# The order of the two halves in the last update of x behind the mixer, and in the squares of the norm that follows

## The chip, the cores and the metric

The kernel runs on one core of a Trainium2 chip. The metric is the device time of one execution in microseconds (us); for the kernel before it is the median of three runs. Everything is float32 or the rounded float32 format (fp32r) that the matrix engine takes.

A core has five engines, each with its own instruction stream, run in the order in which it was built: TensorE (PE in the profile; its weight loads stand as PEld), VectorE (DVE), ScalarE (ACT), GpSimd (POOL) and SyncE (SP), which here issues nearly all DMAs. They wait for one another through semaphores. Matrix products land in PSUM, which has eight banks of 128 x 512 float32; everything else lies in SBUF.

## What is computed

One decoder layer on x (1 x 512 x 1024), in three phases. Each one norms x, runs a block, norms its output, and adds that to x:

```
x = x + 0.5 * PostNorm_a(SwiGLU_1(PreNorm_a(x)))
x = x +       PostNorm_b(W_out [HGRN2_heads(h) ; mLSTM_heads(h)]),  h = PreNorm_b(x)
x = x + 0.5 * PostNorm_c(SwiGLU_2(PreNorm_c(x)))

def rms_norm(x, g):
    xf = x.astype(jnp.float32)
    y = xf * lax.rsqrt(jnp.mean(xf * xf, axis=-1, keepdims=True) + EPS)
    return (y * g.astype(jnp.float32)).astype(x.dtype)

def swiglu_ffn(x, w_in, w_out):
    gate, up = jnp.split(x @ w_in, 2, axis=-1)
    return (jax.nn.silu(gate) * up) @ w_out
```

The change lies where the second phase ends and the third begins: PostNorm_b, the addition to x, PreNorm_c, and the first products of SwiGLU_2.

## The kernel before

**Tiles and precision.** The 512 rows of x are four chunks of 128, held in SBUF as `xs` (128 x 4 x 1024). A chunk's row of 1024 is worked on in two halves of 512: half 0 is columns 0 to 511, half 1 is columns 512 to 1023. Every matrix operand is split into a rounded high part and a remainder: a cast on ACT writes the high part and a subtraction on DVE the rest (lines 245 and 247 for weights, 339 and 341 or 353 and 352 for the normed x). A product is then three matmuls, high by high and the two mixed ones.

**The end of the mixer.** Its output product has two column halves. The first (`mix_out0`) runs for all four chunks, and `post0` leaves its result, times the gain of PostNorm_b, in SBUF as `y` (line 443), with the squares of the first half summed. The second (`mix_out1`) runs chunk by chunk into four banks, `acc[0]` to `acc[3]`. When a chunk's bank is full, `last` (line 468) calls for it, in this order:

1. `post1` (line 446). ACT squares the bank and sums it (line 406, `junk<-ps`). POOL adds this to the sum of half 0 (407) and takes the power -0.5 (411): this is the column `r`. DVE multiplies the bank by the gain in place (453). Then DVE updates x twice (457): half 0 from `y`, which lies in SBUF, and half 1 from the bank, each as x + r * value.
2. `norm(i, 2)`, which is `pre` (414) with `root` (421) and `scaled` (431). ACT squares the two halves of the new x (406, `junk<-xs`) one after the other into the same scratch tile `junk`, POOL makes the root of each sum of squares (407, 407, 411), and DVE scales the two halves by root and gain (433) into `xn` or, for odd chunks, into a part of `hf`.
3. The transposes of the normed chunk on PE (319) and the split of their result into high part and remainder. Those of chunk 0 and chunk 1 are put into the product of chunk 3, those of chunks 2 and 3 into the first products of the third phase (`ffn_head`, line 619).

**The first products of the third phase.** They stand in the list `HEADS`: c1, c3, c2, c4, p1, e1 and so on. c1 to c4 take the first 256 rows, which are chunks 0 and 1; e1 is the first to take chunks 2 and 3. Each is 24 matmuls (line 562). All PSUM tiles come from one ring of eight banks, so a new tile has the bank of the tile eight allocations before it. From `acc[0]` on these are the four `acc`, the four tiles of the transposes of chunks 0 and 1, then c1's, two for the transposes of chunk 2, and c3's.

**Who sets the order.** The code is recorded as a program in which each engine's instructions are put into a sequence by a scheduler of the framework, from the dependences and from what `issue_after` (in `behind`, line 461) forbids. Only the very start of the kernel is written in a fixed order. `post1` and `pre` leave the names of their last square, last update and last scaling in `self.added` and `self.normed`; `ffn_head` puts some weight splits and copies behind them.

`ffn_out` of both SwiGLUs calls `last` too. There `out` is given (a part of `hf`), so neither half is read from a bank in the update, and the norm is called with row 1 or not at all.

Of the kernel before, what the change touches and what calls it, by code (L numbers as in the profile page):

```python
# [87 lines left out]
class Layer:  # L88
# [322 lines left out]
        self.pow = nc.gpsimd.tensor_tensor(r, b, self.nhalf[:, :1], op=ALU.pow)  # L411
        yield r

    def pre(self, i, g):

        r, xn = self.root(i)
        for h in range(2):
            self.scaled(i, g, r, xn, h)
        return xn

    def root(self, i):

        x = self.xs[:, i, :]
        *_, r = self.rms([x[:, :512], x[:, 512:]])
        if i % 2:
            xn = self.hf[:, 16:18, :].rearrange("p a t -> p (a t)")
        else:
            xn = self.sp.tile([P, D], F32, tag="xn", bufs=1, name=self.nm("xn"))
        return r, xn
# [16 lines left out]
    def post1(self, i, y, parts, rms, pieces, g, out=None):  # L446

        nc = self.nc
        for ps, v in pieces:
            parts.append(ps)  # L450
            next(rms)
            o = ps if out is None else out[:, v]
            nc.vector.tensor_tensor(o, ps, g[:, 512 + v.start : 512 + v.stop], op=ALU.mult)
        r = next(rms)
        for h, v in enumerate((y, pieces[0][0] if out is None else out)):
            x = self.xs[:, i, 512 * h : 512 * h + 512]
            added = nc.vector.scalar_tensor_tensor(x, v, r, x, op0=ALU.mult, op1=ALU.add)
        self.added = [self.square, added]
# [1182 lines left out]
def layer(tc, aps):  # L1641
    with ExitStack() as ctx:
        L = Layer(ctx, tc, aps)
        nc = tc.nc
        x, out = aps["x"], aps["out"]
        pre, post = aps["norm_pre"][0], aps["norm_post"][0]
        L.weights(
            L.ffn_items("f1", aps["ffn1_w_in"][0], aps["ffn1_w_out"][0]) + L.mix_items()
            + L.ffn_items("f2", aps["ffn2_w_in"][0], aps["ffn2_w_out"][0])
        )  # L1650
        gp, xn, roots = [None], [None] * NT, {}

        def norm(i, row=None):
            if i == 0 and row is not None:
                gp[0] = L.gain("gpre", pre[row : row + 1, :])
            xn[i] = L.pre(i, gp[0])

        def root(i):

            if i < 2:  # L1660
                norm(i, 1)
            else:
                roots[i] = L.root(i)

        def scaled(i, h):
            r, xn[i] = roots[i]
            L.scaled(i, gp[0], r, xn[i], h)

        def trans(i):
            L.to_t(i, xn[i])  # L1670

        def trans_s(i):
            L.to_s(i, xn[i])

        def store(i):
            for h in range(2):
                v = slice(512 * h, 512 * h + 512)
                nc.sync.dma_start(out[0, i * P : (i + 1) * P, v], L.xs[:, i, v])

        with ExitStack() as f1:  # L1680
            L.open_ffn(f1)
            with tc.manual_schedule():
                first = L.start_loads()
                gp[0] = L.gain_pe("gpre", pre[0:1, :])
                for i in range(NT):
                    for h in range(2):
                        v = slice(512 * h, 512 * h + 512)
                        (nc.scalar if i < 2 and h else nc.sync).dma_start(L.xs[:, i, v], x[0, i * P : (i + 1) * P, v])
                    if i:
                        L.load(first.popleft())  # L1690
                    if i == 1:

                        nc.scalar.activation(L.col(), L.nhalf[:, :1], AF.Exp)
                while first:
                    L.load(first.popleft())
                L.start(norm, xn)
            L.small_params()
            L.ffn_in()
            L.ffn_out(post[0:1, :], 0.5, root, trans, lambda trans: L.head4(trans, scaled))
        L.mixer()  # L1700
        with ExitStack() as f2:
            L.open_ffn(f2)
            L.mix_out1(lambda i: norm(i, 2), trans_s, L.ffn_head)
            L.ffn_in()
            L.ffn_out(post[2:3, :], 0.5, store, lambda i: None, lambda trans: None)
# [30 lines left out]
```

## Time and profile before

| what | value |
| --- | --- |
| median of the runs | 943.95 us (943.27, 943.95, 944.35) |
| the profiled execution | 944.65 us |
| its span, first to last instruction | 942.9 us |
| mean granted clock of PE | 0.999 |
| matmuls | 7507, busy 934.1 us |
| busiest other engine | DVE, 779.7 us |
| output updates of x from a bank (line 457, `xs<-ps`) | 4, at 592.2 to 610.9 us |

The times of the profile are those of one execution, counted from its first instruction. In a row of the timeline stand the start, the duration, the engine, the line in the kernel, the operation, what is written and read, the count of merged instructions, and in brackets the idle time ahead of it with what ended it. In a row of the table of windows each engine has its busy time and the number of its instructions, in the order PE, PEld, DVE, ACT, POOL; then follow the granted clock of PE, the share of the DMA engines, and GB/s. A row of the chain of waits holds the start, the time that the piece adds to the chain, the engine, and what it writes. Matmul ends are modelled, and successive ones overlap in the rows, so their starts say more than their durations.

### The profile page before, as it was taken

The numbers are of one execution on the slowest core, as the hardware profiler recorded it, in microseconds if no ns is written. First come the engines' busy times: TensorE is split into PE (matmuls) and PEld (weight loads), VectorE is DVE, ScalarE is ACT, GpSimd is POOL, SyncE is SP. The second block draws the span as 40 slices with busy tenths as digits, with TensorE's granted clock in tenths as the row PEclk, the third lists the DMA queues.
The fourth block names the chain that finished last, engine by engine and source line by source line (L and its number), as shares of the span: only waits on it lengthen the run. The fifth ranks groups of instructions, "written<-read, shape, count | busy, mean of one in ns | idle before, by whom it ended". The sixth has DMA issues, their size and how long they took to land.

```text
span 942.9 us, 18101 instructions
## 1 busy us (share of the span) xinstructions
PE 934.1 (99%) x7507; PEld 900.4 (95%) x7507; DVE 779.7 (83%) x1056; ACT 490.8 (52%) x695; POOL 120.9 (13%) x176
## 2 busy tenths in 40 slices
PE   9999999999999999999999999999999999999997
PEld 7999999999999999998887888899999999999997
DVE  6799989999888876698846665689998999998884
ACT  7645444456456467956632444664444444655541
POOL 2530000000001046200011310363100000000101
PEclk9999999999999999999999999999999999999999
DMA  9244333323352024321212124324333333223212
GB/s 318 86 135 134 110 116 113 112 90 90 99 171 90 24 85 126 107 67 47 88 46 67 46 90 140 103 71 132 115 113 106 119 113 112 68 90 128 75 46 90
DMA packets 81677, 96.13 MB, mean 102 GB/s; under 512 B 4117, under 2 KB 61497, under 8 KB 81594
## 3 DMA queue, kind: packets, MB, share of 16 engines
q1 hardware_dynamic: 81306, 94.44, 31.7%
q8 instruction: 59, 0.97, 0.4%
q10 hardware_dynamic: 288, 0.52, 0.2%
q14 instruction: 24, 0.20, 0.1%
HBM read 92.85 MB, written 2.10 MB: 101 GB/s over the span
## 4 chain that ended last, share of the span: by engine, by line
PE 62%; ACT 1%; DVE 1%; POOL 0%; issue 0%; POOLq 0%; DVEq 0%; ACTq 0%
PE ps L562 22%; PE ps L835 8%; PE ps L496 6%; PE ps L151 5%; PE ps L843 5%; PE ps L153 4%; PE ps L152 4%; PE ps L1226 2%; PE ps L506 1%; PE ps L319 1%; PE ps L1400 0%; PE ps L1311 0%; PE ps L1480 0%; PE ps L1507 0%; PE ps L1266 0%; ACT junk L406 0%
## 5 line engine op out<-in xcount | busy, mean ns | idle before, releaser
L245 ACT CAST w<-raw 128x1024 fp32r<-128x1024 f32 (+1 forms) x232 | 239.1, 1035 | 252.9 <-PE ps L562 102.5
L247 DVE TENSOR_TENSOR w<-raw,w 128x1024 fp32r<-128x1024 f32 (+1 forms) x232 | 286.1, 1240 | 35.8 <-ACT w L245 35.5
L562 PE MATMUL ps<-xq,w 128*128 128x256 f32 x2016 | 238.5, 277 | 0.0
L562 PEld LDWEIGHTS ps<-xq,w 128*128 128x128 f32 x2016 | 233.8, 188 | 0.2 <-ACT hf L589 0.2
L562 PE MATMUL ps<-sq,w 128*128 128x256 f32 x1440 | 170.5, 277 | 0.0
L562 PEld LDWEIGHTS ps<-sq,w 128*128 128x128 f32 x1440 | 166.8, 188 | 0.0
L835 PE MATMUL ps<-w,hs 128*128 128x256 f32 x1056 | 124.2, 276 | 0.0
L835 PEld LDWEIGHTS ps<-w,hs 128*128 128x128 f32 x1056 | 121.7, 188 | 0.0
L261 DVE TENSOR_TENSOR raw<-raw,raw 128x1024 f32<-128x1024 f32 x64 | 82.3, 1285 | 0.6
L151 PE MATMUL ps<-w,xq 128*128 128x512 f32 x192 | 78.9, 411 | 0.1
L152 PE MATMUL ps<-w,xq 128*128 128x512 f32 x192 | 74.8, 390 | 0.0
L153 PE MATMUL ps<-w,xq 128*128 128x512 f32 x192 | 74.8, 391 | 0.0
L407 POOL TENSOR_SCALAR col<-col 128x1 f32<-128x1 f32 x24 | 9.0, 374 | 493.7 <-ACT junk L406 493.6
L496 PE MATMUL ps<-xq,w 128*128 128x256 f32 x480 | 56.4, 278 | 0.0
L496 PEld LDWEIGHTS ps<-xq,w 128*128 128x128 f32 x480 | 55.2, 188 | 0.5 <-issue 0.5
L843 PE MATMUL ps<-w,hs 128*128 128x256 f32 x432 | 51.9, 276 | 0.0
L261 POOL TENSOR_TENSOR raw<-raw,raw 128x1024 f32<-128x1024 f32 x16 | 44.2, 2763 | 50.7 <-DVE w L247 41.4
L843 PEld LDWEIGHTS ps<-w,hs 128*128 128x128 f32 x432 | 50.3, 188 | 0.0
L754 ACT CAST hs<-hf 128x1024 fp32r<-128x1024 f32 x34 | 35.7, 1050 | 25.7 <-PE ps L843 14.1
L151 PEld LDWEIGHTS ps<-w,xq 128*128 128x128 f32 x192 | 36.1, 188 | 8.2 <-issue 0.9
L153 PEld LDWEIGHTS ps<-w,xq 128*128 128x128 f32 x192 | 36.0, 188 | 8.2 <-DVE xq L326 0.3
L755 DVE TENSOR_TENSOR hs<-hf,hs 128x1024 fp32r<-128x1024 f32 x34 | 41.6, 1224 | 1.5 <-ACT hs L754 1.5
(255 smaller groups left out, 1167.1 us busy)
## 6 DMA issues: line engine op xcount, KB each, us to landing
raw<-in_ffn_w_in_dram SPq DMA_DIRECT2D x88, 512.0 KB, 3.6
raw<-in_ffn_w_out_dram SPq DMA_DIRECT2D x44, 512.0 KB, 4.1
raw<-in_w_mix_in_dram SPq DMA_DIRECT2D x28, 512.0 KB, 3.6
raw<-in_w_mix_out_dram SPq DMA_DIRECT2D x8, 512.0 KB, 3.6
out_dram<-xs SPq DMA_DIRECT2D x8, 256.0 KB, 2.0
xs<-in_x_dram SPq DMA_DIRECT2D x6, 256.0 KB, 7.0
gpost<-in_norm_post_dram SPq DMA_DIRECT2D x3, 512.0 KB, 4.6
gpre<-in_norm_pre_dram SPq DMA_DIRECT2D x2, 512.0 KB, 4.0
```

The source lines that it names most:

```text
L151: mm(ps, sh, mh, start=start, stop=False, **kw)
L152: mm(ps, sh, ml, start=False, stop=False, **kw)
L153: mm(ps, sl, mh, start=False, stop=stop, **kw)
L245: nc.scalar.copy(hi, raw)
L247: self.low = nc.vector.tensor_tensor(lo, raw, hi.bitcast(F32), op=ALU.subtract)
L261: (nc.vector if late else nc.gpsimd).tensor_tensor(o, o, c, op=ALU.add)
L496: mm(ps[:, u0:u1], w[:, a, k, :], self.xop(k, b, u0, u1), start=k + n + m == 0, stop=k == ND - 1 and n == 2, skip_group_check=True,)
L562: self.nc.tensor.matmul(ps[:, c], wb[b][:, k, v], left[d][:, k, :], start=first and a + n + k == 0, stop=n == 2 and k == KH - 1, skip_grou ...
L754: self.nc.scalar.copy(hi, src)
L755: self.nc.vector.tensor_tensor(lo, src, hi.bitcast(F32), op=ALU.subtract)
L835: mm(out, a[kk][:, i * P : (i + 1) * P], w[:, b, kk, QUARTER * v : QUARTER * (v + 1)], start=begin and c == kk == n == 0, stop=kk == 1 and ...
L843: mm(ps[:, QUARTER * c : QUARTER * (c + 1)], A[a][:, c], B[b], start=begin and c == n == 0, stop=n == 2, skip_group_check=True,)
```

## The change

The second of the two updates in `post1` and the first square in the norm behind it trade places with their neighbours, where the update reads a bank. In `post1`, with no `out` given, the half in the bank (half 1) stands first in the code and the half in SBUF second. The norm in front of the third phase, and only this one (row 2), lists half 1 first among its squares. What is computed is the same sum in the other order of its two parts; no instruction is added or removed. The name kept in `self.added` is now that of the update of half 0, and in `self.normed` that of the square of half 0.

```diff
-    def pre(self, i, g):
+    def pre(self, i, g, turned=False):
 
-        r, xn = self.root(i)
+        r, xn = self.root(i, turned)
...
-    def root(self, i):
+    def root(self, i, turned=False):
 
         x = self.xs[:, i, :]
-        *_, r = self.rms([x[:, :512], x[:, 512:]])
+        parts = [x[:, :512], x[:, 512:]]
+        *_, r = self.rms(parts[::-1] if turned else parts)
...
         r = next(rms)
-        for h, v in enumerate((y, pieces[0][0] if out is None else out)):
+
+        for h, v in ((1, pieces[0][0]), (0, y)) if out is None else ((0, y), (1, out)):
             x = self.xs[:, i, 512 * h : 512 * h + 512]
             added = nc.vector.scalar_tensor_tensor(x, v, r, x, op0=ALU.mult, op1=ALU.add)
         self.added = [self.square, added]
...
-            xn[i] = L.pre(i, gp[0])
+            xn[i] = L.pre(i, gp[0], row == 2)
```

## The prediction

> **What bounds the kernel now.** The page first: TensorE (PE) is busy in all but a hundredth of the span, at full clock.
>
> ```profile
> PE 934.1 (99%) x7507; PEld 900.4 (95%) x7507; DVE 779.7 (83%) x1056; ACT 490.8 (52%) x695; POOL 120.9 (13%) x176
> PEclk9999999999999999999999999999999999999999
> ```
>
> So only what makes PE wait can change the time. The change touches one place, the end of the mixer's output product and the three norms and products behind it, about 590 to 620 us. I asked there for PE's waits, for three windows, and for PE's own rows.
>
> ```profile
> PE ps L562 <- ACT junk L406: 0.4, 1, 0.4
> ...
> 600.00:620.00 20.00, 19.64 (x146) 18.27 (x145) 16.41 (x23) 17.16 (x32) 8.90 (x14) 1.00 0.30 99
> 620.00:640.00 20.00, 20.00 (x176) 20.00 (x176) 18.41 (x22) 10.82 (x18) 10.16 (x4) 1.00 0.03 8
> 640.00:930.00 290.00, 290.00 (x2558) 290.00 (x2557) 262.00 (x320) 141.04 (x181) 16.74 (x19) 1.00 0.32 102
> ...
> 607.56 3.00 PE L562 MATMUL ps<-xq,sq 128*128 128x256 f32 x24
> 610.39 1.03 PE L319 MATMUL ps<-ident,xn 128*128 128x128 f32 x8
> 611.79 3.08 PE L562 MATMUL ps<-xq,sq 128*128 128x256 f32 x24 [0.36 <-ACT junk L406]
> ```
>
> PE waits once, 0.36 us, ahead of the product c3 at 611.79. Behind it PE is busy 20.00 of 20 and 290.00 of 290 us: what is lost at 611.79 has no idle time to be made up in, and what is won there is kept. The third thing to see is who holds c3 back. Its bank is the one that acc[3] of the output product had (eight banks in rotation), and the built program has the product wait for VectorE's (DVE's) last update of x, which reads that bank; the name ACT in the row is only the event that came last. The chain of waits says the same: it leaves PE for the square at 600.61 and comes back to PE only with c3.
>
> ```profile
> 600.61 0.70 ACT junk L406 x2
> ...
> 602.88 0.76 DVE xs L457
> ...
> 607.11 1.42 DVE xn L433 x2
> ...
> 609.73 0.61 DVE ps L453
> 610.34 0.66 DVE xs L457
> ```
>
> Read: square for chunk 2, its update of x, its scaling (xn; its squares and root lie between), and then DVE without a gap until the update of chunk 3. Everything that makes a chunk's norm later goes straight into c3.
>
> **The change part by part.** It adds and removes no instruction. It asks for two moves, per chunk of the second product: on DVE the update of the half in the bank first, and on ScalarE (ACT) the square of that half first. Building the changed kernel and comparing the order on each engine gives the fact on which my forecast rests: **DVE's order is unchanged.** Its scheduler still puts the y update first, in all four chunks. GpSimd (POOL) and SyncE are unchanged, PE has the same matmuls. Only ACT moves: the first square now waits for the second update, and the second one waits only for the first square. In chunk 2 a weight cast (raw_660) goes ahead of the first square and another (raw2_604) between the squares.
>
> The price of one chunk comes from chunk 0, ACT's and DVE's rows:
>
> ```profile
> 592.34 0.63 ACT L406 ACTIVATE junk<-xs 128x512 f32<-128x512 f32 x1 [1.96 <-DVE xs L457]
> 593.14 0.63 ACT L406 ACTIVATE junk<-xs 128x512 f32<-128x512 f32 x1
> ...
> 591.50 0.75 DVE L457 SCALAR_TENSOR_TENSOR xs<-y,col,xs 128x512 f32<-128x512 f32 x1 [0.38 <-POOL col L411]
> 592.17 0.75 DVE L457 SCALAR_TENSOR_TENSOR xs<-ps,col,xs 128x512 f32<-128x512 f32 x1
> 594.98 1.42 DVE L433 SCALAR_TENSOR_TENSOR xn<-xs,col,gpre 128x512 f32<-128x512 f32 x2 [2.07 <-POOL col L411]
> ...
> 597.20 0.75 DVE L457 SCALAR_TENSOR_TENSOR xs<-y,col,xs 128x512 f32<-128x512 f32 x1 [0.19 <-POOL col L411]
> ...
> 600.67 1.41 DVE L433 SCALAR_TENSOR_TENSOR hf<-xs,col,gpre 128x512 f32<-128x512 f32 x2 [2.06 <-POOL col L411]
> ```
>
> The first square starts 0.09 after the update it waits for has ended (592.25 to 592.34), the second 0.80 after the first. The updates start 0.67 apart (592.17 - 591.50). So both squares, the root and the scaling come **0.67 us later in each chunk**: chunk 0's scaling at 595.65 in place of 594.98, ending 597.07.
>
> Does it add up from chunk to chunk? POOL's rows decide, with two of DVE ahead of them:
>
> ```profile
> 611.56 1.22 DVE L247 TENSOR_TENSOR sq<-raw,sq 128x1024 fp32r<-128x1024 f32 x1
> 612.69 1.22 DVE L247 TENSOR_TENSOR w<-raw,w 128x1024 fp32r<-128x1024 f32 x1
> ...
> 595.95 0.58 POOL L407 TENSOR_SCALAR col<-col,col 128x1 f32<-128x1 f32 x1 [1.00 <-ACT junk L406]
> ...
> 601.40 0.82 POOL L407 TENSOR_SCALAR col<-col,col 128x1 f32<-128x1 f32 x1 [0.76 <-ACT junk L406]
> ...
> 606.18 0.26 POOL L407 TENSOR_SCALAR col<-col,col 128x1 f32<-128x1 f32 x1 [1.45 <-ACT junk L406]
> ...
> 611.89 2.07 POOL L407 TENSOR_SCALAR col<-col 128x1 f32<-128x1 f32 x1 [2.37 <-ACT junk L406]
> ```
>
> The small POOL operation of 0.26 us takes 0.58 and 0.82 where it meets the scaling of the chunk before, and ends 0.13 to 0.14 behind it (596.53 after 596.40, 602.22 after 602.08). The next update follows 0.80 after that scaling's end both times (597.20, 602.88). So a later scaling makes the next chunk's update as much later, and each chunk adds its own 0.67.
>
> The Trainium skill (SBUF — State Buffer, "Who interferes with whom") says that a VectorE instruction with two inputs in SBUF and a GpSimd instruction that reads SBUF exclude each other, whoever issues first keeping the ports for the whole instruction. The rows agree that POOL stands still; but by that rule it gets in between the two halves of a scaling, and the sum would be rival 1's.
>
> Chunks 1 to 3 then go by these rows:
>
> ```profile
> 603.73 0.63 ACT L406 ACTIVATE junk<-xs 128x512 f32<-128x512 f32 x1 [1.47 <-DVE xs L457]
> 604.36 1.03 ACT L245 CAST w<-raw 128x1024 fp32r<-128x1024 f32 x1
> 605.29 0.63 ACT L406 ACTIVATE junk<-xs 128x512 f32<-128x512 f32 x1
> 605.92 1.05 ACT L339 CAST xq<-ps 128x512 fp32r<-128x512 f32 x2
> 606.87 1.06 ACT L245 CAST w<-raw 128x1024 fp32r<-128x1024 f32 x1
> ...
> 603.94 1.04 PE L319 MATMUL ps<-ident,hf 128*128 128x128 f32 x8
> ...
> 608.45 1.28 DVE L341 TENSOR_TENSOR xq<-ps,xq 128x512 fp32r<-128x512 f32 x2
> 610.90 0.75 DVE L457 SCALAR_TENSOR_TENSOR xs<-ps,col,xs 128x512 f32<-128x512 f32 x1
> 611.08 0.63 ACT L406 ACTIVATE junk<-xs 128x512 f32<-128x512 f32 x1 [0.66 <-DVE xs L457]
> ```
>
> - Chunk 1: update at 597.87, scaling +1.34, at 602.01. Its transposes are wanted on PE at 603.94, after its end at 603.42: hidden.
> - Chunk 2: update +1.34, at 604.22; first square +2.01. I cost the moved casts at nothing. One cast stood between the two squares before as well (605.29 - 603.73 = 1.56, kept). raw_660's fills the 1.47 us in which ACT waited for the update; its data and slot are there, since it ran at 604.36 without a wait of its own, and it would push the squares only if it started later than 604.8. raw2_604's would start at 606.36, 0.51 ahead of its old 606.87; the rows show its data there only by 606.87, so it could cost up to 0.5, and gain nothing. I take nothing, because at 606.87 too ACT came to it without a wait. So squares, root, scaling (607.11), and ACT's casts of chunk 1 (605.92) all come 2.0 later.
> - Chunk 3: DVE runs from 607.11 to its update without a gap, so the update that reads the bank moves from 610.90 to 612.91, its end from 611.65 to 613.66, and c3, 0.14 behind it, from 611.79 to 613.80.
>
> PE meets this in three pieces. c1, at 607.56, needs ACT's first cast of chunk 1, now at 607.92 and half of 1.05 long: about 1.0 us. Its first 16 matmuls take two thirds of 2.83 (607.56 to 610.39), to 610.4, and its last eight need DVE's remainder of the same cast (608.45, now 610.45, some 0.7 long): 0.75. They end near 612.15, the transposes 1.03 later, and c3 waits 0.6 more. Together 2.35, less the 0.36 that was idle before: 2.0 again.
>
> Three rows bound what lies behind c3:
>
> ```profile
> 619.71 1.07 ACT L353 CAST xq<-ps 128x512 fp32r<-128x512 f32 x2
> 623.24 1.05 ACT L245 CAST w<-raw 128x1024 fp32r<-128x1024 f32 x1 [1.96 <-PE ps L562]
> ...
> 623.97 5.60 PE L562 MATMUL ps<-xq,sq 128*128 128x256 f32 x48
> ```
>
> Nothing there should add to it. ACT's squares of chunk 3 are 0.67 later still (2.67), but their root is not: at 611.89 POOL stands 2.07 us behind two DVE splits, and gets free with these, 2.0 later. ACT carries the 0.67 until it idles before 623.24; e1 at 623.97, now 625.98, uses its casts of 619.71, which would end by 623.45.
>
> **Sum: +2.0 us**, against the profiled execution 944.65 to 946.65; that one lies 0.70 above the median, so I predict 943.95 + 2.0 = **945.95**.
>
> **Rivals.**
> 1. POOL slips in between the halves of a scaling. Its operation then ends before that scaling does, and the next update stands behind DVE's own work alone: 1.33 for the scaling and 0.61 for the product with the gain (609.73), 597.59 in chunk 1 in place of 597.87. Twice 0.28 less: +1.45, 945.4. For it: in chunk 1 POOL would now come at 595.95 into the first half (595.65), not the second as before. Against it: at 611.89 it came into the first of two adjoining DVE splits (611.56, 612.69) and left 0.05 after the second.
> 2. Not slower: DVE does take the bank's half first, as the diff asks. Then the squares start when they did, the bank is free 0.67 earlier, and c3's idle 0.36 goes: 943.6. It decides from the moment the two updates change places; against it stands the built order, in which they don't.
> 3. A delay behind c3 that I call hidden isn't: ACT's extra 0.67 reaches PE. +2.7, 946.65. For it: ACT is without a gap there. Against it: the 2.5 us that e1 leaves.
>
> ```profile
> 941.00:943.00 2.00, 0.00 (x0) 0.00 (x0) 0.00 (x0) 0.00 (x0) 0.00 (x0) 0.72 0.24 91
> ```
>
> 4. The three gaps on PE lower its clock, as in the row above, 0.72 after PE had long stopped. At that clock six us of products would take 2.3 more: +4.3, 948.25. Against it: each gap is at most 1.0 us, and the 0.36 us left 1.00 in the window.
>
> **How the numbers follow.** The runs spread over 943.27 to 944.35, so 0.2%, 1.89 us, is about what a measurement here can tell from no change, and my forecast lies on that line. Chances: forecast 0.70 (0.48 of it above the line), rival 1 0.15 (0.02), rival 2 0.05 (0.03 of it over 0.2% faster, as the spread allows), rival 3 0.08, rival 4 0.02. So faster 0.03, within 0.37, slower 0.60. The range takes in rivals 1 and 3 with half a microsecond of spread below and a third above: 944.8 to 947.0.
>
> **What would show it.** Right: in the profile after, DVE's updates in the old order; the first square of chunk 0 at about 593.0, the scalings later by 0.67, 1.34 and 2.0; PE waiting before c1, within c1 and before c3, and full behind. Wrong: POOL's operation at 595.95 ending before the scaling (rival 1); the update from ps first (rival 2); new waits of PE behind 615 us (rival 3); a granted clock under 1.00 at 608 to 625 (rival 4).

## The result, and the profile after

The kernel after takes **945.33 us** in the median of 16 runs (944.68 to 947.97), the one before 943.83 (943.27 to 945.64, 16 runs): a ratio of 1.0016, 95% interval 1.0010 to 1.0023, or **+1.5 us**. It is slower, and by less than the +2.0 of the forecast. The profiled execution took 945.23 us, its span is 943.5 us.

In the kernel after the lines have moved: the scalings are line 434 (before: 433), the product with the gain 454 (453), the updates of x 459 (457), the large products 564 (562).

First TensorE's row of the page, then the table of windows after (the columns as before), then PE's waits in 600 to 620 us (in total, times, longest).

```profile
PE 934.0 (99%) x7507; PEld 899.9 (95%) x7507; DVE 778.1 (82%) x1056; ACT 490.7 (52%) x695; POOL 118.9 (13%) x176
```

```profile
600.00:620.00 20.00, 18.61 (x135) 16.82 (x134) 15.78 (x22) 15.78 (x30) 7.33 (x14) 1.00 0.27 85
620.00:640.00 20.00, 20.00 (x178) 20.00 (x177) 18.96 (x23) 11.79 (x19) 10.82 (x4) 1.00 0.06 22
640.00:930.00 290.00, 290.00 (x2557) 290.00 (x2556) 260.61 (x320) 141.47 (x181) 15.54 (x19) 1.00 0.32 101
```

```profile
PE ps L564 <- DVE xq L341: 0.6, 1, 0.6
PE ps L564 <- DVE xs L459: 0.5, 1, 0.5
PE ps L564 <- ACT xq L339: 0.3, 1, 0.3
```

One wait of PE has become three, of 1.39 us together; behind 620 us PE is full as it was, at a granted clock of 1.00 in all three stretches. The wait that was put down to ACT's square in front of c3 now has the name of what the product really waits for, the update that reads the bank (line 459). PE's own rows of the timeline, of after:

```profile
607.28 2.10 PE L564 MATMUL ps<-xq,sq 128*128 128x256 f32 x16 [0.30 <-ACT xq L339]
609.95 1.21 PE L564 MATMUL ps<-xq,sq 128*128 128x256 f32 x8 [0.56 <-DVE xq L341]
610.99 1.03 PE L319 MATMUL ps<-ident,xn 128*128 128x128 f32 x8
612.55 3.06 PE L564 MATMUL ps<-xq,sq 128*128 128x256 f32 x24 [0.53 <-DVE xs L459]
...
624.56 5.60 PE L564 MATMUL ps<-xq,sq 128*128 128x256 f32 x48
```

c1 comes in two pieces, c3 waits 0.53, and e1 at 624.56 waits for nothing.

c3 at 612.55 is only 0.76 us behind the 611.79 of before, and the loss is 1.5. The two executions differ ahead of this place as well. So all distances from here on are counted from one event in front of everything that the change moves: ACT's square of the bank of chunk 0. The first row is that of the timeline of before, the fence behind it shows ACT's and DVE's rows of after.

```profile
589.69 0.60 ACT L406 ACTIVATE junk<-ps 128x512 f32<-128x512 f32 x1 [2.78 <-PE ps L153]
```

```profile
588.95 0.60 ACT L406 ACTIVATE junk<-ps 128x512 f32<-128x512 f32 x1 [2.78 <-PE ps L153]
...
592.26 0.63 ACT L406 ACTIVATE junk<-xs 128x512 f32<-128x512 f32 x1 [2.63 <-DVE xs L459]
...
590.75 0.75 DVE L459 SCALAR_TENSOR_TENSOR xs<-y,col,xs 128x512 f32<-128x512 f32 x1 [0.39 <-POOL col L411]
591.42 0.75 DVE L459 SCALAR_TENSOR_TENSOR xs<-ps,col,xs 128x512 f32<-128x512 f32 x1
594.92 1.42 DVE L434 SCALAR_TENSOR_TENSOR xn<-xs,col,gpre 128x512 f32<-128x512 f32 x2 [2.75 <-POOL col L411]
...
596.87 0.73 DVE L459 SCALAR_TENSOR_TENSOR xs<-y,col,xs 128x512 f32<-128x512 f32 x1
...
601.02 1.42 DVE L434 SCALAR_TENSOR_TENSOR hf<-xs,col,gpre 128x512 f32<-128x512 f32 x2 [2.76 <-POOL col L411]
...
602.97 0.73 DVE L459 SCALAR_TENSOR_TENSOR xs<-y,col,xs 128x512 f32<-128x512 f32 x1
...
607.87 1.42 DVE L434 SCALAR_TENSOR_TENSOR xn<-xs,col,gpre 128x512 f32<-128x512 f32 x2 [2.31 <-POOL col L411]
...
611.67 0.74 DVE L459 SCALAR_TENSOR_TENSOR xs<-ps,col,xs 128x512 f32<-128x512 f32 x1
```

The y update still stands first (590.75), the one from the bank second (591.42), and ACT's first square now waits 2.63 us for the second one in place of 1.96. In distances from the bank's square:

| event | before | after | later by | forecast |
| --- | --- | --- | --- | --- |
| scaling of chunk 0 | 5.29 | 5.97 | 0.68 | 0.67 |
| first update of chunk 1 | 7.51 | 7.92 | **0.41** | 0.67 |
| scaling of chunk 1 | 10.98 | 12.07 | 1.09 | 1.34 |
| first update of chunk 2 | 13.19 | 14.02 | **0.83** | 1.34 |
| scaling of chunk 2 | 17.42 | 18.92 | 1.50 | 2.0 |
| update of chunk 3 from the bank | 21.21 | 22.72 | 1.51 | 2.0 |
| c3 | 22.10 | 23.60 | **1.50** | 2.0 |

Each norm does add its 0.67 (0.68, then 0.41 to 1.09, then 0.83 to 1.50). On the way from a scaling to the next update some of it is given back, 0.27 and 0.26 us. POOL's rows of after and the chain of waits show how:

```profile
595.20 0.60 POOL L407 TENSOR_SCALAR col<-col,col 128x1 f32<-128x1 f32 x1 [0.32 <-ACT junk L406]
595.89 0.86 POOL L411 TENSOR_TENSOR col<-col,nhalf 128x1 f32<-128x1 f32 x1
...
600.97 0.27 POOL L407 TENSOR_SCALAR col<-col,col 128x1 f32<-128x1 f32 x1
601.33 0.86 POOL L411 TENSOR_TENSOR col<-col,nhalf 128x1 f32<-128x1 f32 x1
```

```profile
594.92 1.42 DVE xn L434 x2
596.34 0.61 DVE ps L454
596.95 1.32 DVE xs L459 x2
...
601.02 1.42 DVE hf L434 x2
602.44 0.61 DVE ps L454
603.05 1.32 DVE xs L459 x2
```

In chunk 1 (the rows at 595) POOL's small operation starts inside the first half of the scaling (594.92 to 595.67) and ends at 595.80, 0.13 behind that half, not behind the second one at 596.34. In chunk 2 (the rows at 601) it has run at 600.97, before the scaling starts at 601.02, and only the power behind it runs into the scaling. Both times POOL is done before DVE is: the update follows the scaling and the product with the gain without a wait, and its row has lost the bracket "0.19 <-POOL col L411" that it had in before. POOL's operation of chunk 1 did not move when the scaling did: it stands at 6.25 after (595.20 - 588.95) and at 6.26 before (595.95 - 589.69). ACT's square of the next bank, which releases it, waits for PE in both executions and starts 5.46 behind the bank's square of chunk 0 in both (594.41 after, 595.15 before). So a scaling that is 0.68 later meets the operation with its first half in place of its second.

### The profile page after: what moved, and what is told of

It is laid out like the page before. It is cut to its first block, busy times and chain, and to the rows that moved or that the text cites. A ratio compares the mean times of both kernels' runs of the same rounds, so it can differ in the third digit from the quotient of the medians.

```text
span 943.5 us, 18103 instructions
## 1 busy us (share of the span) xinstructions
PE 934.0 (99%) x7507; PEld 899.9 (95%) x7507; DVE 778.1 (82%) x1056; ACT 490.7 (52%) x695; POOL 118.9 (13%) x176
## 4 chain that ended last, share of the span: by engine, by line
PE 60%; DVE 1%; ACT 1%; issue 0%; POOL 0%; POOLq 0%; DVEq 0%; ACTq 0%
PE ps L564 22%; PE ps L837 7%; PE ps L498 6%; PE ps L845 5%; PE ps L151 4%; PE ps L153 4%; PE ps L152 4%; PE ps L1228 2%; PE ps L508 1%; DVE xs L459 1%; ACT junk L406 1%; PE ps L319 1%; PE ps L1402 0%; PE ps L1313 0%; PE ps L1509 0%
## 5 line engine op out<-in xcount | busy, mean ns | idle before, releaser
L261 DVE TENSOR_TENSOR raw<-raw,raw 128x1024 f32<-128x1024 f32 x64 | 80.0, 1250 | 0.6
```

The lines of the kernel that those rows point to most:

```text
L261: (nc.vector if late else nc.gpsimd).tensor_tensor(o, o, c, op=ALU.add)
```

## The experiments

Every experiment is changed against the kernel after, if nothing else is said. c3's place is its distance from the bank's square of chunk 0 (before 22.10, after 23.60). The first three ran beside 29 runs of before with a median of 943.88 us.

**The two halves of the change.** First the updates alone, then the squares alone.

```diff
-            xn[i] = L.pre(i, gp[0], row == 2)
+            xn[i] = L.pre(i, gp[0])
```

> Only the updates of x trade places in the code; the norm squares its halves as before. The built program has the instructions of every engine in the order of the kernel before, so all theories expect 0.0 us against it (943.8, within the spread of its runs), the update from y first in the profile, and c3 about 22.1 us after the square of chunk 0's bank. Any loss over 0.5 us would say that the loss of 1.5 us does not come from the squares.

Measured: 943.83 us (943.37 to 946.15, 12 runs), ratio 0.9999 (0.9991 to 1.0008); c3 at 610.99 - 588.89 = 22.10. The order that the source gives to the two updates has no effect that these runs show.

```diff
-        for h, v in ((1, pieces[0][0]), (0, y)) if out is None else ((0, y), (1, out)):
+        for h, v in enumerate((y, pieces[0][0] if out is None else out)):
```

> Only the norm lists half 1 first among its squares; the updates stand as before. If the squares carry the whole loss: +1.5 us (945.3), c3 some 23.6 us after the square of chunk 0's bank, the same as with the whole change. If the order of the updates in the code costs something by itself, for example through the names kept for later waits: less than +1.2 us.

Measured: 944.98 us (944.59 to 946.85, 11 runs), ratio 1.0013 (1.0004 to 1.0021); c3 at 611.97 - 588.38 = 23.59. PE's rows of that kernel have the same three waits as after:

```profile
606.71 2.10 PE L564 MATMUL ps<-xq,sq 128*128 128x256 f32 x16 [0.29 <-ACT xq L339]
609.36 1.22 PE L564 MATMUL ps<-xq,sq 128*128 128x256 f32 x8 [0.55 <-DVE xq L341]
...
611.97 3.07 PE L564 MATMUL ps<-xq,sq 128*128 128x256 f32 x24 [0.51 <-DVE xs L459]
```

In time this is 1.1 us above before, less than the 1.2 below which the expectation would have seen a cost of the updates' order by itself; the interval, 0.4 to 2.0 us, takes in both 1.1 and 1.5. What decides is the profile, with c3 at 23.59 beside 23.60 and the same waits, and updates_only, which shows no loss: the turned squares carry the whole of it.

**What the change asks for, enforced.** The update of the half in SBUF is put behind the one in the bank; some splits of the normed x are held behind it too, so that DVE's order is otherwise that of before.

```diff
+        self.xq_late = False
...
-                for _ in range(3):
-                    next(g)
+                with self.behind(*(self.added[1:] if self.xq_late else [])):
+                    for _ in range(3):
+                        next(g)
...
+        added = None
         for h, v in ((1, pieces[0][0]), (0, y)) if out is None else ((0, y), (1, out)):
             x = self.xs[:, i, 512 * h : 512 * h + 512]
-            added = nc.vector.scalar_tensor_tensor(x, v, r, x, op0=ALU.mult, op1=ALU.add)
+            with self.behind(*([added] if added and out is None else [])):
+                added = nc.vector.scalar_tensor_tensor(x, v, r, x, op0=ALU.mult, op1=ALU.add)
...
+        self.xq_late = True
```

> The whole change, with the two updates of x held in the new order by an issue constraint, so that VectorE does take the half in the bank first; the split of chunks 0 and 1 is held behind the update of chunk 2, where it stood before. Theory: the loss came only from an order on ScalarE that VectorE did not follow. Then the squares start when they did before, and c3's bank is free 0.67 us earlier: c3 about 21.5 to 21.8 us after the square of chunk 0's bank (22.1 before), PE's wait of 0.36 us ahead of it gone, -0.3 to -0.6 us (943.2 to 943.5). Rival: an update that reads a bank first delays the second or the squares (for example because it stands right behind the product into the same bank and must wait for that to be written): then c3 is at 22.1 us or later, and the time is 943.8 or more.

Measured: 943.36 us (942.93 to 944.6, 11 runs), ratio 0.9989 (0.9980 to 0.9997): 0.5 us less than before, and 1.6 less than squares_only. Its timeline, in which the lines have moved again (463 are the updates, 568 the products):

```profile
590.18 0.75 DVE L463 SCALAR_TENSOR_TENSOR xs<-ps,col,xs 128x512 f32<-128x512 f32 x1 [0.38 <-POOL col L413]
590.84 0.74 DVE L463 SCALAR_TENSOR_TENSOR xs<-y,col,xs 128x512 f32<-128x512 f32 x1
...
609.12 0.75 DVE L463 SCALAR_TENSOR_TENSOR xs<-ps,col,xs 128x512 f32<-128x512 f32 x1
...
609.08 1.03 PE L320 MATMUL ps<-ident,xn 128*128 128x128 f32 x8
610.02 3.04 PE L568 MATMUL ps<-xq,sq 128*128 128x256 f32 x24
```

Now `ps` comes before `y`, no wait is marked at c3, and it stands at 610.02 - 588.38 = 21.64, 0.46 earlier than in before. The starts say more than the missing mark. c3 still starts 0.15 behind the end of the update that reads its bank (609.12 + 0.75 = 609.87), as it did in before (0.14 behind 611.65). From the start of the transposes ahead of it to its own it is 0.94 us here and 1.40 in before (610.39 to 611.79), where transposes that nothing delays take 0.79 (617.43 to 618.22 in before). So PE lost 0.61 ahead of c3 in before, of which the row shows 0.36, and about 0.15 is still lost here.

**One chunk at a time.** The source order of the updates is that of before, and only one chunk's squares are turned (0, 1 or 2 in the condition); one run each, for its profile. The slip theory is rival 1: POOL is done early, and the next update stands behind DVE's own work.

```diff
-            xn[i] = L.pre(i, gp[0], row == 2)
+            xn[i] = L.pre(i, gp[0], row == 2 and i == 0)
```

> Half 1 squared first in the norm of chunk 0 alone. Read is the distance from the square of chunk 0's bank to c3 (22.10 us before, 23.60 with the whole change). Each chunk adds its 0.67 (the forecast): 22.77. GpSimd gets in between the halves of the scaling: chunk 1's update is bound by VectorE's own work, +0.41 in place of 0.67, and chunk 2's by +0.15, so 22.25.

Measured: c3 at 611.86 - 589.62 = 22.24. POOL's and DVE's rows around the next update:

```profile
595.59 1.42 DVE L434 SCALAR_TENSOR_TENSOR xn<-xs,col,gpre 128x512 f32<-128x512 f32 x2 [2.75 <-POOL col L411]
...
597.54 0.74 DVE L459 SCALAR_TENSOR_TENSOR xs<-y,col,xs 128x512 f32<-128x512 f32 x1
...
595.87 0.61 POOL L407 TENSOR_SCALAR col<-col,col 128x1 f32<-128x1 f32 x1 [0.32 <-ACT junk L406]
```

The scaling is 0.68 later, POOL is through at 596.48, 0.14 behind the first half, and the update stands at 7.92, which is +0.41. In chunk 2 the same thing happens a second time: +0.14 is left.

> Half 1 squared first in the norm of chunk 1 alone. By the forecast 22.77. If GpSimd gets in between the halves: chunk 1's scaling 0.67 later, chunk 2's update behind VectorE's own work at +0.45, so 22.55.

Measured: c3 at 22.51, the first update of chunk 2 at 13.61, +0.42. POOL's operation came at 602.29, just behind the scaling's start at 602.26, and was through at 603.07, 0.06 behind the first half.

> Half 1 squared first in the norm of chunk 2 alone, with the casts of weights moved as in the whole change. Both theories: chunk 2's scaling 0.67 later and everything of VectorE behind it to the update of chunk 3, so 22.77. If the moved casts cost something of their own: up to 23.3.

Measured: c3 at 22.75. Behind chunk 2's scaling DVE is without a gap, and the full 0.65 arrives. The forecast gave 22.77 for each of the three chunks; only the last one has it. The three losses, 0.14, 0.41 and 0.65, are 1.20 together and not the 1.50 of the whole change, since each of the two steps from a chunk to the next gives back its 0.27 once and no more.

**Nothing to get in between.** Each chunk's scaling as one instruction of 128x1024, once on the kernel before (wide_before, with the same edit less `turned`) and once on the whole change (wide_after, shown). The expectations name chunks 0 to 2; chunk 3's, behind c3, is in one piece too. The order on every engine is otherwise as it was.

```diff
-    def pre(self, i, g, turned=False):
+    def pre(self, i, g, turned=False, wide=False):
 
         r, xn = self.root(i, turned)
+        if wide:
+            scaled = self.nc.vector.scalar_tensor_tensor(xn, self.xs[:, i, :], r, g, op0=ALU.mult, op1=ALU.mult)
+            self.normed = [self.square, scaled]
+            return xn
         for h in range(2):
             self.scaled(i, g, r, xn, h)
...
-            xn[i] = L.pre(i, gp[0], row == 2)
+            xn[i] = L.pre(i, gp[0], row == 2, row == 2)
```

> The kernel before, with the scaling of chunks 0 to 2 as one 128x1024 instruction in place of two of 128x512; squares in the old order. The order on every engine is otherwise that of before. Distances are from ACT's square of chunk 0's bank (before: c3 at 22.10). One scaling of 128x1024 with a column took 1.28 us, the two halves 1.42, so each scaling ends 0.14 earlier. Both theories (POOL gets in only between two instructions of DVE; POOL stands behind the whole scaling anyway): POOL came into the second half in before, so it is held to the end in both, the updates stay 0.80 behind the scaling's end, and come 0.14 and 0.28 earlier in chunks 1 and 2; chunk 3's update from the bank 0.42 earlier, at 20.79 in place of 21.21. c3 gains only what was idle, 0.36: at 21.74, and the time 0.4 below before. A base for wide_after.

Measured: 943.34 us (942.7 to 944.19, 10 runs) beside 943.73 for before, ratio 0.9995 (0.9986 to 1.0005); c3 at 610.29 - 588.58 = 21.71, without a marked wait, but again 0.14 behind the end of the update (609.40 + 0.75).

> The whole change, with the scaling of chunks 0 to 2 as one 128x1024 instruction. Theory (POOL got in between the two halves): there is nothing to get in between now. Chunk 0's scaling at 5.97 ends at 7.25, POOL's small operation that comes at 6.25 lasts to about 7.38, and the update of chunk 1 starts 0.80 behind the scaling, at 8.05 (after: 7.92). In chunk 1 the power is held behind the whole scaling (13.48) and the update comes 0.72 to 0.80 behind it, near 14.24; c3 near 23.68, which is 1.9 later than wide_before: the forecast's 0.67 per chunk, added up. Rival (the halves have nothing to do with it, POOL simply comes earlier and gets through): the updates come 0.61 behind the scaling's end, at 7.86 and 13.90, and c3 at 23.34, 1.6 later than wide_before. Time by the theory 1.6 above before, by the rival 1.2.

Measured: 945.02 us (944.2 to 946.9, 10 runs), ratio 1.0016 (1.0006 to 1.0025); c3 at 611.58 - 588.10 = 23.48, 1.77 later than in wide_before. The theory said 1.9 and the rival 1.6, so the sum lies between them; its two updates tell more:

```profile
594.06 1.28 DVE L418 SCALAR_TENSOR_TENSOR xn<-xs,col,gpre 128x1024 f32<-128x1024 f32 x1 [2.75 <-POOL col L411]
...
596.15 0.75 DVE L463 SCALAR_TENSOR_TENSOR xs<-y,col,xs 128x512 f32<-128x512 f32 x1 [0.19 <-POOL col L411]
...
602.13 0.74 DVE L463 SCALAR_TENSOR_TENSOR xs<-y,col,xs 128x512 f32<-128x512 f32 x1
...
594.35 1.13 POOL L407 TENSOR_SCALAR col<-col,col 128x1 f32<-128x1 f32 x1 [0.32 <-ACT junk L406]
...
600.27 0.27 POOL L407 TENSOR_SCALAR col<-col,col 128x1 f32<-128x1 f32 x1
600.62 1.40 POOL L411 TENSOR_TENSOR col<-col,nhalf 128x1 f32<-128x1 f32 x1
```

In chunk 1 POOL's operation that took 0.60 in after takes 1.13: it is held to 595.48, 0.14 behind the whole scaling, the bracket of POOL is back, and the update stands at 8.05, as the theory said and 0.67 behind wide_before's 7.38. So the forecast's price is carried on in full where POOL's operation comes into a scaling of one piece. In chunk 2 the theory's 14.24 is wrong: the update is at 14.03 (602.13 - 588.10). There the small operation starts ahead of the scaling (600.27 before 600.32), and the power behind it, held in the scaling, ends only 0.41 after it (602.02 after 601.61), inside DVE's product with the gain. The give-back of chunk 2 does not need the halves, then: the small operation's getting ahead is enough.

**The port by itself.** Two small kernels, which leave out the layer's computation: DVE runs stretches of eight adjoining instructions, and POOL a row of small operations that read SBUF beside them.

> Not the layer: the kernel loads x twice, runs 8 adjoining VectorE products of 128x512 with two operands in SBUF and a column (the kind of the scaling), 8 adjoining differences of 128x1024 with two operands in SBUF (the kind of the split), 8 products of 128x512 with one operand in a bank, while GpSimd runs 75 operations on one column; it leaves out the whole computation of the layer. If GpSimd is held until a run of adjoining VectorE instructions ends (as the forecast had it): in the first two stretches one GpSimd operation lasts about as long as the whole stretch, over 4 us. If it gets in between two of them: operations of at most about 0.8 us in the first stretch and about 1.2 us in the second, one for each VectorE instruction or two. If the two kinds differ, the first shows short ones and the second one long one. In the third all take their 0.2 us.

DVE's stretches (start, length of all eight), and then POOL's operations in the first stretch and in the second (minimum, median and maximum in ns):

```profile
13.58 5.38 DVE L102 SCALAR_TENSOR_TENSOR o<-x,r,g 128x512 f32<-128x512 f32 x8
18.88 9.16 DVE L105 TENSOR_TENSOR o<-x,g 128x1024 f32<-128x1024 f32 x8
```

```profile
L98 POOL TENSOR_SCALAR c<-c x6: 579/701/9784, 15.1 to 18.3; 128x1 f32<-128x1 f32 x6
...
L98 POOL TENSOR_SCALAR c<-c x1: 9784/9784/9784, 18.3 to 18.3; 128x1 f32<-128x1 f32 x1
```

Beside the scalings POOL gets through one operation per instruction of DVE, 0.70 us each. Beside the subtractions, which adjoin just as closely, one operation lasts 9.78 us, to the end of the stretch; it is also the last of the six in the first row. It began at 18.31, inside the last scaling (18.21 to 18.95), and did not get in ahead of the first subtraction either, so a scaling with a column does not by itself let POOL in behind it. Beside products with an operand in a bank an operation takes 0.19. Two things differ between the first two stretches, the size and the column that the scaling takes as its scalar:

> Not the layer: only loads of x and five stretches of 8 adjoining VectorE instructions, with GpSimd operations on one column beside them; the layer's computation is left out. The stretches: products with a column as scalar, 128x1024; products with one operand in a bank; differences, 128x512; products with one operand in a bank; products with a constant as scalar, 128x512. If length decides whether GpSimd gets in between two adjoining instructions: one long GpSimd operation (about 9 us) in the first stretch, short ones in the third and fifth. If the kind of instruction decides: short ones (about 1.2 us) in the first, one long one (about 5 us) in the third, short ones in the fifth. If the column as scalar decides: short ones in the first, long ones in the third and fifth.

```profile
13.69 9.65 DVE L101 SCALAR_TENSOR_TENSOR o<-x,r,g 128x1024 f32<-128x1024 f32 x8
...
28.03 4.91 DVE L109 TENSOR_TENSOR o<-x,g 128x512 f32<-128x512 f32 x8
...
37.62 4.91 DVE L105 SCALAR_TENSOR_TENSOR o<-x,g 128x512 f32<-128x512 f32 x8
```

```profile
L98 POOL TENSOR_SCALAR c<-c x7: 1113/1233/1233, 15.1 to 22.2; 128x1 f32<-128x1 f32 x7
...
L98 POOL TENSOR_SCALAR c<-c x1: 4915/4915/4915, 28.1 to 28.1; 128x1 f32<-128x1 f32 x1
...
L98 POOL TENSOR_SCALAR c<-c x1: 4913/4913/4913, 37.7 to 37.7; 128x1 f32<-128x1 f32 x1
```

The size makes no difference: with a column and 1024 wide POOL gets in after each instruction, 1.23 us apart; without a column and 512 wide it is held through all eight, 4.92 us. The last stretch shown is the scaling's own operation with a constant in place of the column, and POOL is held again, 4.91 us. In these stretches POOL gets in between two instructions that both have a column, and between none without; each kernel has one execution.

## Why the prediction was right in its direction and too high by half a microsecond

**Right: the built order decides, not the source.** DVE's updates stand as before, and updates_only is before to 0.01% with c3 at the same 22.10. The gain that the change could bring was left in the source; bank_first has it, 0.5 us, with c3 0.46 earlier. Rival 2 named the point from which it decides, and bank_first is where it does; its price, 0.36, is the idle time of the row, which shows less than PE had lost. Why the scheduler puts the y update first was not tried.

**Right: 0.67 per chunk, by ACT's wait for the later update.** The first scaling is 0.68 later, and the three steps from an update to its own scaling are 0.68, 0.68 and 0.67.

**Wrong: "So a later scaling makes the next chunk's update as much later, and each chunk adds its own 0.67."** This is the mis-sized term. The carry from a scaling to the next update is 0.27 and 0.26 us short, and the sum is 3 x 0.67 - 0.53 = 1.48 in place of 2.0. The two rows of before on which the step rested (595.95 and 601.40) showed POOL held to the end of the whole scaling, but both came into its second half, where the end of the instruction and the end of the scaling are the same thing. A scaling 0.67 later met POOL's operation with its first half, or had it in front. Rival 1 had the mechanism for chunk 1, and its update at 597.59, counted on after's clock, is 596.85 against the measured 596.87. For chunk 2 it had the amount without needing its reason: wide_after keeps that give-back without any halves, because POOL's operation is in front of the scaling there. So rival 1's sum, +1.45, lies nearer to the measured 1.50 than the forecast's, and the sign that the prediction had named for it did show: POOL's operation of chunk 1 ended at 595.80, before the scaling's end at 596.34. The chances went wrong with the same term: 0.60 stood on a loss over 0.2%, and it is 0.16%.

The row that spoke against rival 1 (611.89, held through two adjoining splits) was of another kind: those splits have no column as a scalar. That the column makes this difference is shown in the small kernels. The kernels of the layer do not follow it everywhere: at that same pair of splits POOL was held through both in six kernels (before, updates_only, chunk0_only, chunk1_only, wide_before, wide_after) and got in between in three (after, squares_only, bank_first). In chunk2_only the two splits do not adjoin. It is not how far into the first split POOL comes: at 0.33 or 0.34 us it was held in before (611.89) and got in in bank_first (610.79), and at about 1.0 us it was held in wide_after (612.37) and got in in after (613.34). What decides there is open.

The rule of the Trainium skill (SBUF — State Buffer, "Who interferes with whom"), one instruction at a time, gave rival 1's sum, and the trace of after agrees with it at 595.80, 0.13 behind the first half. The stretches without a column do not: one operation of POOL was held through eight instructions.

**Right: PE meets it in three pieces.** Ahead of c1 it was 0.46 (forecast about 1.0), within c1 0.78 (0.75), ahead of c3 0.53 (0.6), less the old 0.36: 1.41. The other 0.1 lies in c1's last eight matmuls, which take 1.04 from their start to that of the transposes (609.95 to 610.99), where a third of before's 2.83 is 0.94. Only the first is off, by the half microsecond that ACT's casts of chunk 1 were early. The idle time of the windows (1.39 in place of 0.36) shows only 1.03 of the 1.50, because the last matmul ahead of a break has a modelled end that covers up to 0.2 us of it: 16 matmuls take 2.10 in the row, and two thirds of 2.83 is 1.89. Differences of starts do not have this error.

**Right: moved casts at nothing, and nothing behind c3.** The cast between chunk 2's squares costs what it did: they start 1.57 apart (604.48 and 606.05), before 1.56. From c3 to the end of the span it is 331.1 us before and 331.0 after. Rival 3 would have needed a wait of PE behind 615 us, and rival 4 a granted clock under 1.00; the windows show neither.

## What to carry to other kernels

Where a scheduler sets the order, two edits that lean on each other must be looked up one by one in the built program: here one was undone, and the other, made for an order that did not come, cost 0.67 us in each of three chunks, 1.5 us in all after what came back. An operation that is seen to end behind a pair of instructions has not been shown to wait for the pair; ask in which of the two it started, before a delay is carried on in full. And count distances from the last event that the change cannot move, since two profiled executions were 0.74 us apart before it had any effect.

## What the runs showed of the hardware

- In the small kernels DVE's instructions with both operands in SBUF and no column as scalar held one small operation of POOL through a whole run of eight: 9.78 us (128x1024 subtractions, and the end of the scaling ahead of them), 4.92 (128x512) and 4.91 (the scaling's operation with a constant). Between two instructions with a column POOL got in each time, operations of 0.70 us (512) or 1.23 us (1024). The pair of splits in the layer went both ways.
- A column costs DVE a little: eight adjoining 128x512 instructions took 5.38 us with it and 4.91 with a constant, about 0.06 us from one start to the next. With no operation of POOL beside it, the step from one half of a scaling to the other is as long, 0.67 us (607.11 in before: 1.42 for both, 0.75 for one), so POOL's getting in is not what takes the time. Whether that gap is what lets POOL in was not tried.
- The scaling in one instruction of 128x1024 took 1.28 us, in two halves 1.42.
